# Hybrid attention and delta-rule layer: the delta gates of three groups as half products, another head, other planner constants

## The chip, the core and the metric

The kernel runs on one core of one Trainium2 chip. The metric is the device time of one execution in microseconds (us); the time before is the median of three runs. The engines are TensorE (PE, with its weight loads shown as PEld), VectorE (DVE), ScalarE (ACT), GpSimd (POOL) and SyncE (SP, which issues most DMAs).

## The reference, cut

One decoder layer on 512 tokens of width 1024, with 16 meta tokens in front (528 in all). Attention and a gated delta rule run on the same normalised stream; each is gated, projected, gated again, and merged.

```python
hn = rms_norm(h, norm_w)
proj = hn @ w_in
aq, ak, av, az, dq, dk, dv, dz, db, da, ga, gd = jnp.split(proj, offs, axis=-1)
...
o_a = diff_attention(qa, ka, va, lam)
y_a = (o_a * jax.nn.silu(az)) @ w_branch_attn
...
qkv = jax.nn.silu(causal_depthwise_conv(qkv, conv_w))
o_d = gated_delta_chunked(q, k, v, beta, g)
o_d = rms_norm(o_d[:, pad:], dn_norm_w).reshape(B, L, DN_WIDTH)
y_d = (o_d * jax.nn.silu(dz)) @ w_branch_delta
merged = jax.nn.sigmoid(ga) * y_a + jax.nn.sigmoid(gd) * y_d
return merged @ w_out
```

The layer's output is added to the input and normalised once more; the meta tokens are dropped. All is float32.

## The kernel before

**Dense products.** The columns of w_in are taken in blocks of 128 (one head of aq, ak, av, az, dq, dk, dv or dz, or 128 columns of a merge gate ga or gd). ORDER lists the blocks: four groups of two heads, each with dk, dv, dq, dz and the attention blocks, then gd, ga and the branch products yd and ya. The 1024 rows of a block are 8 pieces of 128. To keep float32 precision, each operand is split into a high and a low part of the faster type float32r (wh and wl for weights, hnH and hnL for the normalised stream), and three products are summed: high by high, high by low, low by high (PASSES). A plain block (`product`) is thus 8 x 3 matmuls for each token segment; for dz, az, aq, ga and gd one segment of 512 tokens (BODY), without the meta tokens.

**Half products.** `pair_of_blocks` computes two neighbouring blocks together, by Strassen's scheme in Winograd's form: the weights of the two blocks, the two halves of the 1024 rows and the two halves of the 528 tokens (264 each) make a 2x2 by 2x2 product, done in seven products in place of eight. Each is 4 pieces x 3 passes of 264 columns. `split_pair` makes the weight sums: four DVE operations of 512 columns, then four high parts on ACT and four low parts on DVE (wa, wb, wc of 1024 columns, wd of 512). The sums over tokens (sumH, sumL) are made once by `token_sums`. Partial results leave PSUM by two snapshots (`snap`) and one into cn (`snap_c`) on ACT, and four additions (`total`) on DVE, into two of four buffers xp (or vT for attention). Then a `whole_...` function takes the block from there. PAIRS says which blocks go this way: before the change ak from the second on, dk, dv and dq of the last three groups, and four blocks of gd.

**The gates of the delta rule.** silu of dz is made as (tanh(z/2) + 1) * z, with the factor one half elsewhere. `after_gate` reads z from PSUM: tanh on ACT into one of two buffers th, then, once the old content of the slot of od has been spilled to DRAM, one DVE operation. The delta rule's output is later multiplied onto it (`steps`).

**The planner.** The program is written by a list scheduler that runs on the host (`Plan`). Every piece of work is a generator that yields what it waits for: an engine, an event, a buffer or a PSUM bank. Of all tasks that wait for an engine, the planner issues the one with the earliest start by its own estimates, and at equal starts the lowest rank. HOP, NEAR, SAME and PE_NS are its estimates of the time from engine to engine and of a matmul's fixed part; BIAS adds to the rank of tasks by name. The order it writes on each engine is fixed; the chip then runs each engine in that order, with semaphores between them. Buffers are limited (SLOTS): four raw weight tiles, three pairs of split weights (W), four xp, two th, six PSUM banks beside two of scores.

**The head.** `loads` issues the DMAs of x (four tiles of 128 tokens), of the meta tokens, and of the first weight blocks. `normalise(n)` does, for the meta tokens (n = 0) and for each tile of x (n = 1 to 4): squares with a sum on ACT, mean and eps on DVE, the power -0.5 on POOL (rs), scaling by rs and by the norm weights on DVE (`half`), transposes on PE, and the split into hnH (ACT) and hnL (DVE) in `part`. The norm weights must stand in all 128 partitions: `norm_weights` multiplies a row of ones by the row nrow on PE, into the PSUM tile psc, after eight products of ones that keep PE going. `first_products` then computes dk of heads 0 and 1, over 272 and then 256 tokens; each block goes through its three passes before the next one starts. Its weights are split in `split`.

All of it is issued through the helper at line 238, so the profile names nearly every instruction by that line; tiles tell them apart. psc is the PSUM tile of scores, room holds the gates od and oa, raw the weights as loaded, st the scratch for squares and for weight sums.

Of the kernel before, what the change touches and what calls it, by code (L numbers as in the profile page):

```python
# [33 lines left out]
def dense_order():  # L34
# [7 lines left out]
    for n in range(KB):  # L42
# [14 lines left out]

ORDER = dense_order()

PAIRS = [n for n, (name, i) in enumerate(ORDER) if name == "ak" and i or name == "gd" and i in range(0, 4, 2) or name in ("dk", "dv", "dq") and i > 1 and i % 2 == 0]  # L60
PAIRED = {m for n in PAIRS for m in (n, n + 1)}
HALF = L // 2
PASSES = ((0, 0), (0, 1), (1, 0))
# [14 lines left out]


COLD = 5200  # L80
HOP = {PE: 205.4, DVE: 130, ACT: 104.2, POOL: 90, SP: 0}
NEAR = {PE: 80, DVE: 0, ACT: 0, POOL: 0, SP: 0}
SAME = 81.7
PE_NS = dict(transpose=53, f32=0.1, f32r=11.2, long=18)
BIAS = dict(after_aq=-1.7, after_dv=-0.5, attention=-0.3, combine=0.3, decayed=2, keys=-0.3, move=-2, norms=-1,
            output=2.5, products=-2, quarter=1, rest=1, split=-0.3, split_pair=-0.5, sums=2, values=2.6, whole_av=-1,
            whole_dk=0.3, whole_dq=2)


class Task:  # L90
    def __init__(self, gen, rank, time, src):
        self.gen, self.rank, self.time, self.src, self.want, self.slot = gen, rank, time, src, (), 0
        self.issued = None


class Plan:
# [8 lines left out]
    def __init__(self, slots, kinds, banks):  # L105
        self.free = dict.fromkeys((PE, DVE, ACT, POOL, SP), 0.0)
        self.slots = {k: [(0.0, SP, i) for i in range(n)] for k, n in slots.items()}
        self.slots["bank"] = [(0.0, SP, i) for i in range(banks)]
        self.kinds = dict(kinds)
        self.events, self.tasks = {}, []  # L110
        self.task, self.engine, self.end, self.arrival = None, None, 0.0, 0.0
        self.dma = self.hwdge = 0.0

# [5 lines left out]

    def spawn(self, gen, rank=None):  # L120
        time, src = self.here() if self.task else (0.0, SP)
        rank = (self.task.rank if rank is None else rank) + BIAS.get(gen.__name__, 0)
        self.tasks.append(Task(gen, rank, time, src))

    def done(self, event):
        self.events[event] = self.here()
# [65 lines left out]
    def run(self):  # L192
        self.settle()
        while self.tasks:
            best = None
            for task in self.tasks:
                eng = task.want
                if isinstance(eng, tuple) or eng not in self.free:
                    continue
                t = task.time if task.issued is None or eng != SP else task.issued  # L200
                if task.src != eng:
                    t += HOP[task.src] + NEAR[eng]
                elif eng in (DVE, ACT):
                    t += SAME
                key = max(t, self.free[eng]), task.rank
# [69 lines left out]
def hybrid_block(ctx: ExitStack, tc: tile.TileContext, x, meta, wblk, wbd, wout, pcol, prow, out):  # L275
# [49 lines left out]
        return ticks[event] == n  # L325


    nrow = mk(sp, [1, D], F32, "nrow")
    nc.scalar.dma_start(out=nrow, in_=prow[:, 1296:2320])
    plan.events["nrow"] = 3200.0, SP  # L330
    mt = mk(sp, [P, 2 * P], F32, "mt")
    plan.free.update({ACT: 2000.0, DVE: 1000.0, POOL: 1200.0, SP: 630.0})

# [81 lines left out]
    def split(n, raw, which):  # L415

        m = n - len(ORDER)
        if m < 0 or m in (4, 5):
            if n:
                yield f"took {n - 1 if m != 4 else len(ORDER) - 1}"  # L420
            yield ("W",)
            w_slot[n] = plan.task.slot
            wh, wl = Ws[plan.task.slot]
            done(f"took {n}")
        else:
            yield ("wo",)
            wo_slot[n] = plan.task.slot
            wh, wl = wos[plan.task.slot]
        if n == 1:
            yield "hh2"  # L430
        yield ACT
        A.copy(out=wh, in_=raw)
        weights[n] = wh, wl
        done(f"wh{n}")
        if n == 0:
            yield "scaled 2"
        yield DVE
        V.tensor_tensor(out=wl, in0=raw, in1=wh.bitcast(F32), op=ALU.subtract)
        plan.give("raw", which)
        done(f"w{n}")  # L440
# [75 lines left out]
    def loads():  # L516
        for n in range(1, NC + 1):
            yield SP
            S.dma_start(out=xt[n], in_=x[P * (n - 1):P * n, :])
            done(f"x{n}")  # L520
# [12 lines left out]
        S.dma_start(out=wbr, in_=wbd)  # L533
        done("wbr")
        for n in range(2, len(ORDER) + 8):
            yield from load_weights(n)


    hn = [hnp.tile([P, KB, L], F32R, tag=t, name=t) for t in ("hnH", "hnL")]

    def normalise(n):

        yield f"x{n}"
# [2 lines left out]
        ss, rs = (mk(sp, [P, 1], F32, t, 5) for t in ("ss", "rs"))  # L546
        if n > 2:
            yield "hh2"
        yield ACT
        A.activation(out=st[:, :w], in_=xt[n], func=AF.Square, accum_out=ss)  # L550
        src = ss
        if n == 0:
            yield "same"
# [5 lines left out]
        yield DVE  # L559
        V.tensor_scalar(out=ss, in0=src, scalar1=1.0 / D, scalar2=EPS, op0=ALU.mult, op1=ALU.add)  # L560
        if n == 0:
            give("pdl", pt)
        yield POOL
# [34 lines left out]
            spawn(part(pt, dst, hf), 0.25 + 0.02 * hf)  # L598

        for hf in range(1 if n == 0 else 2):  # L600
            spawn(half(hf))
# [339 lines left out]
    def after_dq(h, banks):  # L941
        pair["q", h], _ = yield from conv_silu(banks, h, NM, "qT")
        give("y")
        done(f"dq{h}")

    def whole_gd(c, which):
        th = xps[which][:, 3 + NM:3 + L]
# [664 lines left out]
    def attention(h):  # L1612
# [129 lines left out]
        if h < H - RING["oa"]:  # L1742
# [8 lines left out]
    WHOLE = dict(dk=whole_dk, dv=whole_dv, dq=whole_dq, ak=whole_ak, av=whole_av, gd=whole_gd)  # L1751
    parts, th_, mg = {}, {}, {}

    def branch(name, of):
# [180 lines left out]
    def first_products():  # L1935

        dst = [[], []]
        banks = [Banks(n) for n in range(2)]
        for hb, (t0, nn) in enumerate(FULL):
            for n in range(2):  # L1940
                if n == 1 and hb == 1:
                    yield ("psc",)
                    dst[1].append(bank("psc")[:, 0])
                else:
                    yield ("pd",)
                    dst[n].append(bank("pd"))
                pd = dst[n][hb][:, :nn]
                for m, (i, j) in enumerate(((0, 0), (1, 0), (0, 1))):
                    yield (f"wh{n}", f"w{n}")[i]
                    for e in (0, 1, 2) if hb == 0 else (3, 4):  # L1950
                        yield f"{('hh', 'hn')[j]}{e}" + ("/0" if j == 0 else "")
                    for k in range(KB):
                        if j == 0 and k == KB // 2:
                            for e in (1, 2) if hb == 0 else (3, 4):
                                yield f"hh{e}/1"
                        yield PE
                        T.matmul(pd, weights[n][i][:, k * P:(k + 1) * P], hn[j][:, k, t0:t0 + nn],
                                 start=k == 0 and m == 0, stop=k == KB - 1 and m == 2)
# [336 lines left out]
            spawn(delta_pair(gi))  # L2295
            yield "ap"

    for task, rank in ((norm_weights(), 0), (loads(), 0), (constants(), 5), (gates(), 0.6), (deltas(), 0), (pools(), 0), (dense(), 4),
                       (token_sums(), 3), (returns(), 1)):
# [52 lines left out]
```

## Time and profile before

| what | us |
|---|---|
| median of three runs | 748.05 |
| lowest and highest | 748.04, 749.8 |
| the profiled execution's own time | 748.15 |
| its span, first to last instruction | 746.4 |

The profile is of one execution. A busy time is the union of an engine's instructions; those of PE overlap each other, since matmuls are pipelined and their ends are modelled. In a table by stretches the columns are the stretch, its length, and for PE, PEld, DVE, ACT and POOL the busy time with the number of instructions; then the clock granted to PE (1.00 is full), the share of the DMA engines, and GB/s. In a row by group, behind the count stand the busy time and the mean of one in ns, and behind the next bar the idle time of the engine before them and what ended it. In a timeline row stand start, length, engine, line, operation, tiles and count.

### The profile page before, as it was taken

Reading aid. Unit: us, or ns where it says so; the run is one execution under the profiler, and the core shown is the slowest. Engines: PE = TensorE matmul, PEld = TensorE weight load, DVE = VectorE, ACT = ScalarE, POOL = GpSimd, SP = SyncE. Lnnn points to the kernel's source line nnn. Section 1 sums busy time; section 2 is a strip of 40 time slices with the busy share of each in tenths; the row PEclk is TensorE's granted clock in tenths of the full one; section 3 lists DMA queues with packets and bytes.
Section 4 is the critical chain, followed back from the end, with each engine's and each line's share of the span. In section 5 each row is a group of like instructions: output and inputs, shape, how many; then the busy total and the mean of one; then the engine's idle time right before and its main releaser. Section 6 shows DMA issues by size and latency. Waiting matters only on the chain.

```text
span 746.4 us, 14531 instructions
## 1 busy us (share of the span) xinstructions
PE 733.6 (98%) x5346; PEld 670.1 (90%) x5346; DVE 624.0 (84%) x1472; ACT 519.0 (70%) x1390; POOL 64.0 (9%) x72
## 2 busy tenths in 40 slices
PE   8999999999999999999999999999999999999996
PEld 7998988899898899889889989989988999899875
DVE  5989998888899988889997798998569767989553
ACT  6449857899977598987668898768785445555232
POOL 2104001003100002200100220010010000000001
PEclk8999999999999999999999999999999999999998
DMA  8233211424243222432233232403273443215603
GB/s 300 67 108 121 87 57 65 99 74 133 79 126 104 55 71 79 133 114 88 98 66 84 86 118 83 142 29 73 93 249 111 154 158 114 85 57 165 203 1 113
DMA packets 51249, 79.11 MB, mean 106 GB/s; under 512 B 21029, under 2 KB 30685, under 8 KB 51178
## 3 DMA queue, kind: packets, MB, share of 16 engines
q1 hardware_dynamic: 51176, 78.18, 33.0%
q8 instruction: 42, 0.69, 0.4%
q14 instruction: 29, 0.24, 0.1%
q10 hardware_dynamic: 2, 0.00, 0.0%
HBM read 70.63 MB, written 7.55 MB: 105 GB/s over the span
## 4 chain that ended last, share of the span: by engine, by line
PE 73%; DVE 15%; ACT 6%; issue 2%; DMA 1%; POOL 1%; SPq 0%; POOLq 0%; DVEq 0%; ACTq 0%
PE bank L238 70%; DVE wl L238 3%; PE psc L238 3%; DVE room L238 2%; DVE ts L238 1%; DVE psc L238 1%; ACT wh L238 1%; DVE vin L238 1%; ACT ak L238 1%; DMA raw<-in_wblk_dram 1%; DVE y L238 1%; DVE sumL L238 1%; ACT e L238 1%; DVE aq L238 1%; DVE ast L238 1%
## 5 line engine op out<-in xcount | busy, mean ns | idle before, releaser
L238 PE MATMUL bank<-hnH,wh 128*128 128x512 f32 (+4 forms) x624 | 218.7, 356 | 0.2
L238 PE MATMUL bank<-hnL,wh 128*128 128x512 f32 (+4 forms) x624 | 207.0, 336 | 0.2 <-DVE ss L238 0.2
L238 PE MATMUL bank<-hnH,wl 128*128 128x512 f32 (+4 forms) x624 | 206.8, 336 | 0.0
L238 DVE TENSOR_TENSOR wl<-raw,wh 128x1024 fp32r<-128x1024 f32 (+1 forms) x124 | 137.1, 1109 | 21.6 <-ACT wh L238 21.0
L238 ACT CAST wh<-raw 128x1024 fp32r<-128x1024 f32 (+1 forms) x124 | 118.5, 958 | 38.9 <-PE bank L238 30.6
L238 PEld LDWEIGHTS bank<-hnH,wh 128*128 128x128 f32 x624 | 117.5, 191 | 12.5 <-issue 0.3
L238 PEld LDWEIGHTS bank<-hnH,wl 128*128 128x128 f32 x624 | 116.9, 190 | 12.5
L238 PEld LDWEIGHTS bank<-hnL,wh 128*128 128x128 f32 x624 | 116.7, 189 | 9.9 <-DVE ss L238 0.4
L238 PE MATMUL bank<-sumH,wh 128*128 128x264 f32 x288 | 88.8, 308 | 0.0
L238 PE MATMUL bank<-sumH,wl 128*128 128x264 f32 x288 | 81.8, 284 | 0.0
L238 PE MATMUL bank<-sumL,wh 128*128 128x264 f32 x288 | 81.7, 284 | 0.0
L238 DVE SCALAR_TENSOR_TENSOR y<-xp,pc,y 128x528 f32<-128x528 f32 (+1 forms) x72 | 54.3, 758 | 1.6 <-ACT y L238 1.3
L238 PEld LDWEIGHTS bank<-sumH,wh 128*128 128x128 f32 x288 | 54.6, 189 | 0.3
L238 PEld LDWEIGHTS bank<-sumL,wh 128*128 128x128 f32 x288 | 54.5, 189 | 0.0
L238 PEld LDWEIGHTS bank<-sumH,wl 128*128 128x128 f32 x288 | 54.2, 188 | 0.0
L238 ACT ACTIVATE e<-psc,ast 128x144 f32<-128x144 f32 (+3 forms) x64 | 34.6, 542 | 17.9 <-DVE ast L238 16.9
L238 DVE TENSOR_TENSOR wl<-st,wh 128x1024 fp32r<-128x1024 f32 x26 | 31.8, 1222 | 7.7 <-ACT wh L238 7.7
L238 PE MATMUL bank<-btH,wh 128*128 128x256 f32 x128 | 36.3, 284 | 0.5 <-ACT sn L238 0.5
L238 POOL TENSOR_TENSOR ass<-ass,mhalf 128x4 f32<-128x4 f32 x8 | 10.1, 1260 | 306.3 <-DVE ass L238 175.1
L238 PE MATMUL bank<-btH,wl 128*128 128x256 f32 x128 | 36.2, 283 | 0.0
L238 PE MATMUL bank<-btL,wh 128*128 128x256 f32 x128 | 36.1, 282 | 0.0
L238 ACT CAST wh<-st 128x1024 fp32r<-128x1024 f32 x26 | 27.3, 1048 | 11.3 <-PE bank L238 10.8
(382 smaller groups left out, 1722.7 us busy)
## 6 DMA issues: line engine op xcount, KB each, us to landing
raw<-in_wblk_dram SPq DMA_DIRECT2D x96, 512.0 KB, 3.6
raw<-in_wout_dram SPq DMA_DIRECT2D x8, 512.0 KB, 4.7
xt<-in_x_dram SPq DMA_DIRECT2D x4, 512.0 KB, 6.7
TE<-gcd SPq DMA_DIRECT2D x8, 256.0 KB, 4.6
TT<-gcd SPq DMA_DIRECT2D x8, 256.0 KB
xr<-in_x_dram SPq DMA_DIRECT2D x8, 256.0 KB, 6.3
out_dram<-xr SPq DMA_DIRECT2D x7, 256.0 KB, 2.3
room<-scrm SPq DMA_DIRECT2D x12, 128.0 KB, 3.7
```

What stands on the lines that cost most here:

```text
L238: return real(*args, **kw)
```

## The change

It has three parts.

The dz blocks of groups 1 to 3 become pairs: PAIRS takes in dz, and `whole_dz` makes the gate from xp instead of PSUM. The blocks of group 0 stay as they are.

The head: nrow is loaded as 8 rows of 128 and transposed once, copied to SBUF as eight columns (nwc), and each column, repeated along the free axis, is transposed into psc. The eight products of ones go; a task of the highest rank (`keep_busy`) issues such products whenever nothing else of PE is ready in the plan, until the first half of hnH of tile 2 is there. The squares of tile 1 are shared by half between ACT and DVE, those of tile 2 by three quarters and one quarter. Tile 2 goes ahead of the meta tokens. The high part of the first weight block is made in two halves, that of the third block waits until tile 4 is scaled. `first_products` goes through its passes in another order.

The planner's constants: HOP, NEAR, SAME, PE_NS and BIAS have other values, and BOOST changes the rank of two single tasks.

```diff
-PAIRS = [... or name in ("dk", "dv", "dq") and i > 1 and i % 2 == 0]
+PAIRS = [... or name in ("dk", "dv", "dq", "dz") and i > 1 and i % 2 == 0]
...
-HOP = {PE: 205.4, DVE: 130, ACT: 104.2, POOL: 90, SP: 0}
-NEAR = {PE: 80, DVE: 0, ACT: 0, POOL: 0, SP: 0}
-SAME = 81.7
-PE_NS = dict(transpose=53, f32=0.1, f32r=11.2, long=18)
-BIAS = dict(after_aq=-1.7, after_dv=-0.5, attention=-0.3, combine=0.3, decayed=2, keys=-0.3, move=-2, norms=-1,
-            output=2.5, products=-2, quarter=1, rest=1, split=-0.3, split_pair=-0.5, sums=2, values=2.6, whole_av=-1,
-            whole_dk=0.3, whole_dq=2)
+HOP = {PE: 100, DVE: 84.9, ACT: 140, POOL: 90, SP: 0}
+NEAR = {PE: 87.2, DVE: 0, ACT: 0, POOL: 0, SP: 0}
+SAME = 120
+PE_NS = dict(transpose=53, f32=0.5, f32r=10.6, long=15.7)
+BIAS = dict(after_dv=-0.5, after_gate=-2.3, after_sigmoid=1.5, combine=-0.3, decayed=-2.8, delta_pair=-1.5,
+            diagonal=-0.5, evac=2.3, keys=1, part=2.5, queries=0.5, rest=0.3, sigmoid=-2, total=-0.2, whole_ak=0.3,
+            whole_dv=1.5)
+BOOST = {"delta_pair 2": 0.7, "split 14": -0.7}
...
-    nrow = mk(sp, [1, D], F32, "nrow")
-    nc.scalar.dma_start(out=nrow, in_=prow[:, 1296:2320])
-    plan.events["nrow"] = 3200.0, SP
+    nrow = mk(sp, [KB, P], F32, "nrow")
+    nc.scalar.dma_start(out=nrow, in_=prow[:, 1296:2320].rearrange("o (k p) -> (o k) p", p=P))
+    plan.events["nrow"] = 2600.0, SP
...
-        if n == 1:
-            yield "hh2"
-        yield ACT
-        A.copy(out=wh, in_=raw)
+        if n in (1, 2):
+            yield ("hh2", "scaled 4")[n - 1]
         weights[n] = wh, wl
+        if n == 0:
+            yield ACT
+            A.copy(out=wh[:, :D // 2], in_=raw[:, :D // 2])
+            done("wh0/0")
+            plan.task.rank += 0.04
+            yield ACT
+            A.copy(out=wh[:, D // 2:], in_=raw[:, D // 2:])
+        else:
+            yield ACT
+            A.copy(out=wh, in_=raw)
...
+    def other_squares(n, m):
+        late["ss", n] = mk(sp, [P, 1], F32, "sx", 2)
+        yield DVE
+        V.tensor_tensor_reduce(out=st[:, m:], in0=xt[n][:, m:], in1=xt[n][:, m:], scale=1.0 / D, scalar=EPS, op0=ALU.mult,
+                               op1=ALU.add, accum_out=late["ss", n])
+        done(f"squares {n}")
...
+        m = {1: D // 2, 2: D // 4 * 3}.get(n, w)
+        if m < w:
+            spawn(other_squares(n, m))
         yield ACT
-        A.activation(out=st[:, :w], in_=xt[n], func=AF.Square, accum_out=ss)
+        A.activation(out=st[:, :m], in_=xt[n][:, :m], func=AF.Square, accum_out=ss)
...
+        if m < w:
+            yield f"squares {n}"
+            yield DVE
+            V.scalar_tensor_tensor(out=ss, in0=ss, scalar=1.0 / D, in1=late["ss", n], op0=ALU.mult, op1=ALU.add)
...
+        nwc = mk(sp, [P, KB], F32, "nwc")
+        yield "nrow"
         yield PE
-        for _ in range(8):
-            T.matmul(late["nw"][0][:, 0:P], ones, ones, start=True, stop=True)
-        yield "nrow"
-        for hf in range(2):
+        T.transpose(nw[:, 1, 0:KB], nrow, ident[0:KB, 0:KB])
+        yield DVE
+        V.tensor_copy(out=nwc, in_=nw[:, 1, 0:KB])
+        for k in range(KB):
             yield PE
-            T.matmul(late["nw"][hf], ones[0:1], nrow[:, 512 * hf:512 * hf + 512], start=True, stop=True)
-            done(f"norm weights {hf}")
+            T.transpose(nw[:, k // 4, k % 4 * P:k % 4 * P + P], nwc[:, k:k + 1].broadcast_to([P, P]), ident)
+            tick(f"norm weights {k // 4}", 4)
+
+    def keep_busy():
+        yield ("pdl",)
+        fill = bank("pdl")
+        while "hh2/0" not in plan.events:
+            yield PE
+            T.matmul(fill[:, 0:P], ones, ones, start=True, stop=True)
+        give("pdl", fill)
...
+    def whole_dz(h, which):
+        z = xps[which][:, 3 + NM:3 + L]
+        yield ("th",)
+        at_ = plan.task.slot
+        th = ths[at_]
+        yield ACT
+        A.activation(out=th, in_=z, func=AF.Tanh, scale=0.5)
+        if h >= RING["od"]:
+            yield f"od out {h - RING['od']}"
+        yield DVE
+        V.scalar_tensor_tensor(out=gate["od"][h], in0=th, scalar=1.0, in1=z, op0=ALU.add, op1=ALU.mult)
+        plan.give("xp", which)
+        plan.give("th", at_)
+        done(f"dz{h}")
...
-            for n in range(2):
-                if n == 1 and hb == 1:
...
+            for n, m in ((0, 0), (0, 1), (1, 0), (0, 2), (1, 1), (1, 2)):
+                i, j = ((0, 0), (1, 0), (0, 1))[m]
...
-    for n, rank in ((1, 0), (0, 0.1), (2, 0.2), (3, 0.4), (4, 0.5)):
+    for n, rank in ((1, 0), (2, 0.02), (0, 0.04), (3, 0.4), (4, 0.5)):
         spawn(normalise(n), rank)
```

More of the change, by code (lines that the diff above doesn't have):

```diff
@@ L58 @@
 ORDER = dense_order()
-PAIRS = [n for n, (name, i) in enumerate(ORDER) if name == "ak" and i or name == "gd" and i in range(0, 4, 2) or name in ("dk", "dv", "dq") and i > 1 and i % 2 == 0]
+PAIRS = [n for n, (name, i) in enumerate(ORDER) if name == "ak" and i or name == "gd" and i in range(0, 4, 2) or name in ("dk", "dv", "dq", "dz") and i > 1 and i % 2 == 0]
 PAIRED = {m for n in PAIRS for m in (n, n + 1)}
@@ L92, in __init__ @@
         self.gen, self.rank, self.time, self.src, self.want, self.slot = gen, rank, time, src, (), 0
-        self.issued = None
+        self.issued, self.boost = None, 0
 class Plan:
@@ L109, in __init__ @@
         self.kinds = dict(kinds)
-        self.events, self.tasks = {}, []
+        self.events, self.tasks, self.count = {}, [], {}
         self.task, self.engine, self.end, self.arrival = None, None, 0.0, 0.0
@@ L121, in spawn @@
         time, src = self.here() if self.task else (0.0, SP)
-        rank = (self.task.rank if rank is None else rank) + BIAS.get(gen.__name__, 0)
+        name = gen.__name__
+        rank = (self.task.rank if rank is None else rank) + BIAS.get(name, 0)
         self.tasks.append(Task(gen, rank, time, src))
+        self.count[name] = self.count.get(name, -1) + 1
+        self.tasks[-1].boost = BOOST.get(f"{name} {self.count[name]}", 0)
     def done(self, event):
@@ L204, in run @@
                     t += SAME
-                key = max(t, self.free[eng]), task.rank
+                key = max(t, self.free[eng]), task.rank + task.boost
                 if best is None or key < best[0]:
@@ L519, in loads @@
             S.dma_start(out=xt[n], in_=x[P * (n - 1):P * n, :])
+            plan.late(1200 if n == 2 else 0)
             done(f"x{n}")
@@ L558, in normalise @@
             src = pt[:, 0:1]
-        yield DVE
-        V.tensor_scalar(out=ss, in0=src, scalar1=1.0 / D, scalar2=EPS, op0=ALU.mult, op1=ALU.add)
+        if m < w:
+            yield f"squares {n}"
+            yield DVE
+            V.scalar_tensor_tensor(out=ss, in0=ss, scalar=1.0 / D, in1=late["ss", n], op0=ALU.mult, op1=ALU.add)
+        else:
+            yield DVE
+            V.tensor_scalar(out=ss, in0=src, scalar1=1.0 / D, scalar2=EPS, op0=ALU.mult, op1=ALU.add)
         if n == 0:
@@ L600, in normalise @@
         for hf in range(1 if n == 0 else 2):
-            spawn(half(hf))
+            spawn(half(hf), {0: 0.13, 1: 0.1, 2: 0.12}.get(n, plan.task.rank) + 0.02 * hf)
     def norm_weights():
@@ L944, in after_dq @@
         done(f"dq{h}")
+    def whole_dz(h, which):
[7 more added lines that the diff above has]
+            yield f"od out {h - RING['od']}"
+        yield DVE
+        V.scalar_tensor_tensor(out=gate["od"][h], in0=th, scalar=1.0, in1=z, op0=ALU.add, op1=ALU.mult)
+        plan.give("xp", which)
+        plan.give("th", at_)
+        done(f"dz{h}")
     def whole_gd(c, which):
@@ L1750, in hybrid_block @@
                  av=lambda h, banks: to_whole(whole_av, h, banks))
-    WHOLE = dict(dk=whole_dk, dv=whole_dv, dq=whole_dq, ak=whole_ak, av=whole_av, gd=whole_gd)
+    WHOLE = dict(dk=whole_dk, dv=whole_dv, dq=whole_dq, ak=whole_ak, av=whole_av, gd=whole_gd, dz=whole_dz)
     parts, th_, mg = {}, {}, {}
@@ L1939, in first_products @@
         for hb, (t0, nn) in enumerate(FULL):
-            for n in range(2):
-                if n == 1 and hb == 1:
[L1942 to L1946, printed above, removed]
-                pd = dst[n][hb][:, :nn]
[L1948 to L1958, printed above, removed]
+            for n, m in ((0, 0), (0, 1), (1, 0), (0, 2), (1, 1), (1, 2)):
+                i, j = ((0, 0), (1, 0), (0, 1))[m]
+                if m == 0:
+                    if n == 1 and hb == 1:
+                        yield ("psc",)
+                        dst[1].append(bank("psc")[:, 0])
+                    else:
+                        yield ("pd",)
+                        dst[n].append(bank("pd"))
+                pd = dst[n][hb][:, :nn]
+                yield ("wh0/0" if m == n == 0 else f"wh{n}", f"w{n}")[i]
+                for e in (0, 1, 2) if hb == 0 else (3, 4):
+                    yield f"{('hh', 'hn')[j]}{e}" + ("/0" if j == 0 else "")
+                for k in range(KB):
+                    if j == 0 and k == KB // 2:
+                        yield f"wh{n}"
+                        for e in (1, 2) if hb == 0 else (3, 4):
+                            yield f"hh{e}/1"
+                    yield PE
+                    T.matmul(pd, weights[n][i][:, k * P:(k + 1) * P], hn[j][:, k, t0:t0 + nn],
+                             start=k == 0 and m == 0, stop=k == KB - 1 and m == 2)
+                if m < 2:
+                    continue
                 done(banks[n].event(hb))
@@ L2296, in deltas @@
             yield "ap"
-    for task, rank in ((norm_weights(), 0), (loads(), 0), (constants(), 5), (gates(), 0.6), (deltas(), 0), (pools(), 0), (dense(), 4),
+    for task, rank in ((norm_weights(), -1), (keep_busy(), 9), (loads(), 0), (constants(), 5), (gates(), 0.6), (deltas(), 0), (pools(), 0), (dense(), 4),
                        (token_sums(), 3), (returns(), 1)):
         spawn(task, rank)
-    for n, rank in ((1, 0), (0, 0.1), (2, 0.2), (3, 0.4), (4, 0.5)):
+    for n, rank in ((1, 0), (2, 0.02), (0, 0.04), (3, 0.4), (4, 0.5)):
         spawn(normalise(n), rank)
```

## The prediction

> **What bounds the kernel now.** First the page: its span, the busy time of each engine, and the chain of work that ended last.
>
> ```profile
> span 746.4 us, 14531 instructions
> PE 733.6 (98%) x5346; PEld 670.1 (90%) x5346; DVE 624.0 (84%) x1472; ACT 519.0 (70%) x1390; POOL 64.0 (9%) x72
> PE 73%; DVE 15%; ACT 6%; issue 2%; DMA 1%; POOL 1%; SPq 0%; POOLq 0%; DVEq 0%; ACTq 0%
> ```
>
> TensorE (PE) is busy for 98% of the span and carries 73% of the chain; VectorE (DVE) is second in both. A busy PE may still be waiting inside its pipeline, so I next read the busy time by stretches.
>
> ```profile
> 100.00:500.00 400.00, 397.17 (x3067) 366.26 (x3066) 358.55 (x930) 323.34 (x952) 40.56 (x36) 1.00 0.31 92
> ...
> sum 715.00, PE 711.00 PEld 650.82 DVE 608.04 ACT 503.64 POOL 55.94; mean PE 177.75 PEld 162.70 DVE 152.01 ACT 125.91 POOL 13.99
> ```
>
> The columns are PE, weight loads, DVE, ACT, POOL, then the granted PE clock. From 20 to 735 us PE is idle for 715.00 - 711.00 = 4.0 us. So three things can shorten this kernel: less matmul work, a shorter head before 20 us, or those 4.0 us; the tail after 735 us is not edited. The head:
>
> ```profile
> 10.00:15.00 5.00, 4.56 (x21) 4.31 (x21) 4.57 (x7) 3.49 (x7) 0.00 (x0) 0.50 0.93 310
> ```
>
> PE is granted half its clock from 10 to 15 us, just where the first products run.
>
> **The gates as half products (PE).** Each of three pairs of dz blocks drops 2 blocks x 8 x 3 = 48 matmuls of 512 columns and gains 7 products x 4 x 3 = 84 of 264. A duration in the trace overlaps its neighbour, so I take steps from start to start, between rows of one uninterrupted run of PE's timeline:
>
> ```profile
> 558.81 0.40 PE L238 MATMUL bank<-hnH,wh 128*128 128x512 f32 x1
> ...
> 564.37 0.40 PE L238 MATMUL bank<-hnH,wh 128*128 128x512 f32 x1
> ```
> ```profile
> 177.53 0.37 PE L238 MATMUL bank<-sumH,wh 128*128 128x264 f32 x1
> ...
> 181.84 0.28 PE L238 MATMUL bank<-sumH,wl 128*128 128x264 f32 x1
> ```
>
> The first two rows lie 24 matmuls apart: 5.56/24 = 0.2317 us. The other two lie 35 apart: 4.31/35 = 0.1231 us. A pair goes from 48 x 0.2317 = 11.12 to 84 x 0.1231 = 10.34 us, which saves 0.78, and three save 2.3 us. (The gain is not one eighth, since half products also run over the 16 meta tokens that dz skipped.) The Trainium skill, TensorE: Matmul & The Clock Gate, section on the back-to-back issue gap, gives a warm step as columns/2.4 plus 2.5 ns; by that a pair would save 0.91 us and the three 2.7, an estimate from the page; the rows here are slower per column than it, and the measurement decides.
>
> **What the gates add on DVE and ACT.**
>
> ```profile
> L238 DVE TENSOR_TENSOR wl<-raw,wh 128x1024 fp32r<-128x1024 f32 x98 | 119.5, 1221 | 19.6 <-ACT wh L238 19.2
> ...
> L238 DVE TENSOR_TENSOR wl<-raw,wh 128x512 fp32r<-128x512 f32 x26 | 17.8, 686 | 2.0 <-ACT wh L238 1.8
> ...
> L238 DVE SCALAR_TENSOR_TENSOR room<-room,bank 128x512 f32<-128x512 f32 x16 | 11.1, 694 | 0.0
> ...
> L238 DVE TENSOR_TENSOR xp<-bank,cn 128x264 f32<-128x264 f32 x22 | 9.5, 431 | 4.5 <-PE bank L238 3.1 <-ACT cn L238 1.3
> ...
> L238 DVE SCALAR_TENSOR_TENSOR qT<-xp,y 128x512 f32<-128x512 f32 x8 | 5.5, 682 | 0.8 <-ACT xp L238 0.8
> ```
> ```profile
> L238 ACT CAST wh<-raw 128x1024 fp32r<-128x1024 f32 x98 | 102.7, 1048 | 36.4 <-PE bank L238 30.6 <-DVE raw L238 2.3 <-DVE room L238 1.7
> ...
> L238 ACT CAST wh<-raw 128x512 fp32r<-128x512 f32 x26 | 16.1, 620 | 2.5 <-DVE raw L238 2.4
> ...
> L238 ACT ACTIVATE room<-bank 128x512 f32<-128x512 f32 x19 | 11.3, 596 | 0.0
> ...
> L238 ACT COPY xp<-bank 128x264 f32<-128x264 f32 x22 | 8.4, 381 | 2.3 <-PE bank L238 2.0
> ...
> L238 ACT ACTIVATE xp<-y 128x512 f32<-128x512 f32 x8 | 5.0, 629 | 0.7 <-DVE y L238 0.7
> ```
>
> DVE loses, per pair, two splits and two gates from PSUM: 2 x 1.22 + 2 x 0.69 = 3.83 us. It gains four weight sums (half a split's size, so its price), three and a half splits, four totals and two gates from SBUF: 4 x 0.686 + 3 x 1.221 + 0.686 + 4 x 0.431 + 2 x 0.682 = 10.18. Net +6.35 a pair, 19 us in all. ACT goes from 2 x 1.048 + 2 x 0.596 = 3.29 to 3 x 1.048 + 0.620 + 3 x 0.381 + 2 x 0.629 = 6.16: +2.9 a pair (cn's snap priced as the other two). Loads and spills stay as many. The dz pair holds two of the four xp buffers where the block held PSUM banks; the pair of dk behind it takes the other two. The spill of the old od slot is waited for as before.
>
> What hides 6.35 us of DVE? The first three rows are the dz blocks as they stand; the next three run on through the pair behind them; the last is a long stretch.
>
> ```profile
> 241.20:254.30 13.10, 13.10 (x68) 10.92 (x66) 12.66 (x47) 6.74 (x25) 1.80 (x3) 1.00 0.06 21
> 367.60:381.00 13.40, 13.40 (x66) 10.87 (x66) 13.16 (x53) 6.40 (x21) 0.00 (x0) 1.00 0.07 28
> 490.70:505.20 14.50, 14.50 (x79) 12.29 (x78) 14.06 (x55) 8.19 (x27) 2.23 (x3) 1.00 0.00 0
> 241.20:273.00 31.80, 31.65 (x275) 28.37 (x273) 28.44 (x86) 23.50 (x78) 1.80 (x3) 1.00 0.21 51
> 367.60:400.00 32.40, 31.98 (x273) 28.20 (x273) 27.42 (x85) 22.40 (x67) 0.00 (x0) 1.00 0.22 55
> 490.70:523.00 32.30, 32.30 (x279) 29.00 (x278) 29.03 (x94) 24.10 (x79) 2.23 (x3) 1.00 0.19 42
> ```
> ```profile
> 200.00:250.00 50.00, 50.00 (x342) 45.89 (x341) 48.67 (x137) 37.08 (x101) 2.22 (x3) 1.00 0.32 101
> ```
>
> In the dz blocks themselves DVE is nearly full: free 0.4, 0.2 and 0.4 us. To the end of the next pair it has 3.4, 5.0 and 3.3 us free, so 1.4 to 3.1 us of each 6.35 is carried further as lateness. The cover is other DVE work that can slide (attention, the delta rule) while PE takes what is ready. It holds in the last row: DVE 97% busy for 50 us, PE never idle. The bounds of the cost: below, 0 by that row; above, all that the longer stretches don't cover, 3.0 + 1.4 + 3.1 = 7.5 us, or without any sliding 19. Over 100:500 DVE's free time falls from 41.5 to some 24 us; were PE's 2.83 us idle there to grow in that ratio, it would gain 2. I take **+0.8 us**, nearer the 50 us row. ACT's 2.9 us lie in its own gaps: it is busy 6.7 of 13.1, 6.4 of 13.4 and 8.2 of 14.5 us in the dz blocks, so 0; without that cover they would add to DVE's lateness, at most 2.9 each.
>
> **The head.**
>
> ```profile
> 1.15 3.78 PE L238 MATMUL psc<-ones 128*128 128x128 f32 x16 [1.15 <-DVE ones L238]
> ...
> 4.86 2.02 PE L238 MATMUL psc<-nrow,ones 1*128 1x512 f32 x4
> ...
> 7.00 1.41 DVE L238 SCALAR_TENSOR_TENSOR xt<-xt,rs,psc 128x512 f32<-128x512 f32 x2 [1.14 <-PE psc L238]
> ...
> 8.56 1.07 POOL L238 TENSOR_TENSOR rs<-ss,mhalf 128x1 f32<-128x1 f32 x2 [2.06 <-DVE ss L238]
> ...
> 9.66 1.41 DVE L238 SCALAR_TENSOR_TENSOR xt<-xt,rs,psc 128x512 f32<-128x512 f32 x2 [0.17 <-POOL rs L238]
> ...
> 10.46 1.97 PE L238 MATMUL bank<-ident,xt 128*128 128x128 f32 x8 [0.44 <-DVE xt L238]
> ...
> 12.25 2.18 PE L238 MATMUL bank<-hnH,wh 128*128 128x272 f32 x8
> ...
> 17.12 1.17 PE L238 MATMUL bank<-hnH,wh 128*128 128x272 f32 x8
> ...
> 18.34 2.72 DVE L238 SCALAR_TENSOR_TENSOR xt<-xt,rs,psc 128x512 f32<-128x512 f32 x4
> ```
> ```profile
> 7.00:19.00 12.00, 10.57 (x55) 8.92 (x54) 10.18 (x18) 8.39 (x16) 3.40 (x6) 0.72 0.89 320
> ```
>
> Scaling of x1 starts at 7.00, released by the norm-weight matmuls that end at 6.88. Instead come one transpose, a DVE copy and eight transposes. Eight transposes took 1.97 us at half clock in the row at 10.46; so from 4.86 at the latest the weights are there by about 7.3 at half clock, some 1 us sooner at full, and sooner still if the row of weights lands earlier, since the 16 warming matmuls no longer stand before it. Halved squares of x1 make rs earlier as well. I take 6.3 for x1. For x2 the power no longer stands behind that of the meta tokens (two took 1.07, so 0.53 sooner), the squares lose a quarter, and x1's scaling before it is 0.7 earlier: start near 8.2 instead of 9.66. The first matmul then comes near 10.5 instead of 12.25.
>
> Whether that is kept depends on the feed. At full clock the first eight matmuls take 1.2 us as in the row at 17.12, not 2.18; but from 7 to 19 us DVE was busy 10.18 of 12 and the second scaling (x3, x4) came only at 18.34. DVE gets added squares, priced by 0.69 us for 512 columns and half that for 256, and a small copy: 1.2 us, out of 1.8 idle. The fillers use PE only while nothing else is ready in the plan, and one of two pdl banks until the first half of hnH of x2; one filler call is two of the matmuls of ones, of which 16 took 3.78 us, so 0.5 us if it stands before work that came early. Bounds: a loss of 0.5 (late weights, or one filler too many) to a gain of 3 (start and clock both kept). I take **-1.8 us**, the earlier start. Splitting wh0 costs ACT one fixed part, 2 x 0.620 - 1.048 = 0.2 us; the reorder of the first products gives DVE time for the low parts and changes no count.
>
> **The constants** change the order that the planner writes, not the work. The most to gain is the 4.0 us of idle; at the other end a worse order can cost as much. I take 0, with 1.5 us either way.
>
> **The sum.** -2.3 - 1.8 + 0.8 = -3.3 us. The profiled execution took 748.15 us (span 746.4), the median of three is 748.05, so both are one base: **744.7 us**.
>
> **Rivals.**
> 1. *Better still:* head 2.8 us, no DVE price, the new order takes 1 to 2 of the idle: 748.05 - 2.3 - 2.8 - 1.5 = 741.5. For it: the half clock. Chance 0.17.
> 2. *The head doesn't do what it says:* fillers end before the hn tiles come and the clock still falls, or DVE paces the head. Gain 0: 748.05 - 2.3 + 0.8 = 746.6. For it: DVE's 10.18 of 12. Chance 0.11.
> 3. *DVE becomes the bound at the dz pairs, slower than before:* its 6.35 us lateness reaches PE through the weight splits, of which only three buffers stand ahead. With 7.5 us arriving: 748.05 - 4.1 + 7.5 = 751.5; with all 19: 763. It is slower by over 0.3% once 6.3 of the 19 us reach PE. Against it: the row with DVE at 97%. Chance 0.18, more than half of it above 750.3.
> 4. *Weight loads bind.* If loads ran one after another, each half product would cost a load, not 0.123 us.
>
> ```profile
> L238 PEld LDWEIGHTS bank<-sumH,wh 128*128 128x128 f32 x288 | 54.6, 189 | 0.3
> ```
> ```profile
> 204.00:209.00 5.00, 5.00 (x44) 5.00 (x43) 5.00 (x15) 3.08 (x9) 0.00 (x0) 1.00 0.81 252
> ```
>
> At 0.189 us a pair would take 84 x 0.189 = 15.9 instead of 11.12, three +14.3: 748.05 - 1.8 + 0.8 + 14.3 = 761. But 43 loads in 5.00 us of half products are one per 0.116 us: they overlap. Chance 0.02. [...]
>
> **How the numbers follow.** About 0.3%, 2.2 us, is what a measurement can tell from no change. The forecast has 0.52, 0.43 of it below 745.8. Faster: 0.43 + 0.17 = 0.60. Same: 0.09 + 0.11 + 0.08 = 0.28. Slower: 0.10 + 0.02 = 0.12. The range goes from the better case to where the DVE price is some 5 us: 741.2 to 749.5, leaving out about 0.05 below and 0.14 above.
>
> **What would show it.** In the new trace: the rows of 128x512 matmuls fall by 144 and those of 264 rise by 252, steps unchanged; the clock of 10:15 near 1.00; first product near 10.5 and PE unbroken from about 17; DVE busy near 640; PE idle of 20:735 within 3.5 to 6.5. Idle of PE ended by DVE's wl or st in the dz stretches would make me wrong by rival 3; a half clock after 8 us by rival 2.

## The result, and the profile after

| kernel | median of 6 runs, us | lowest, highest | profiled execution, us | span, us |
|---|---|---|---|---|
| before | 749.59 | 748.04, 750.10 | 748.15 | 746.4 |
| changed | 744.72 | 744.22, 745.59 | 744.65 | 742.9 |

Both were timed together on one chip: ratio 0.9937, 95% interval 0.9926 to 0.9947. The change is faster by some 0.6%. The forecast was 744.7 us. Several of its terms were wrong all the same, and cancelled. Two of the six executions of the kernel before took 748.0 us and the others 749.4 to 750.1, so its profiled one is among the fastest: the medians differ by 4.9 us, the profiled executions by 3.5.

The page of the changed kernel, its span and busy times, then the chain:

```profile
span 742.9 us, 14923 instructions
...
PE 731.9 (99%) x5499; PEld 677.3 (91%) x5499; DVE 638.0 (86%) x1507; ACT 522.9 (70%) x1406; POOL 57.9 (8%) x72
...
PE 85%; ACT 9%; DVE 2%; DMA 2%; issue 2%; SPq 0%; POOL 0%; POOLq 0%; DVEq 0%; ACTq 0%
```

PE is still the bound, now with 85% of the chain. DVE works 14 us more (638.0 against 624.0) and yet carries 2% of the chain instead of 15%. The busy time by stretches (PE, weight loads, DVE, ACT, POOL, then PE's clock), the head's stretch first:

```profile
7.00:19.00 12.00, 12.00 (x104) 11.80 (x103) 10.43 (x22) 8.00 (x16) 3.16 (x6) 1.00 0.97 324
...
100.00:500.00 400.00, 397.36 (x3188) 373.46 (x3187) 371.31 (x971) 322.67 (x945) 34.70 (x34) 1.00 0.31 93
...
20.00:735.00 715.00, 711.24 (x5353) 657.37 (x5351) 622.92 (x1471) 510.25 (x1380) 50.97 (x50) 1.00 0.33 101
```

PE's idle time from 20 to 735 us is 715.00 - 711.24 = 3.8 us (4.0 before), and from 100 to 500 us DVE is busy for 371 of 400 us instead of 359 with PE no idler than it was. The groups of PE's instructions, each form apart, first of the kernel before and then of the changed one:

```profile
L238 PE MATMUL bank<-hnL,wh 128*128 128x512 f32 x288 | 114.0, 396 | 0.0
...
L238 PE MATMUL bank<-sumH,wh 128*128 128x264 f32 x288 | 88.8, 308 | 0.0
...
L238 PE MATMUL bank<-hnL,wh 128*128 128x264 f32 x216 | 61.3, 284 | 0.0
```
```profile
L242 PE MATMUL bank<-sumH,wh 128*128 128x264 f32 x336 | 102.9, 306 | 0.0
...
L242 PE MATMUL bank<-hnL,wh 128*128 128x512 f32 x240 | 94.8, 395 | 0.0
...
L242 PE MATMUL bank<-hnL,wh 128*128 128x264 f32 x252 | 71.5, 284 | 0.0
```

Each of the three kinds of 512-column matmul fell from 288 to 240, and the half products rose from 288 and 216 to 336 and 252: 144 fewer and 252 more, as worked out. The mean times are within 2 ns of those before.

Now the head: DVE's timeline of the changed kernel (start, duration), then ACT's, then PE's.

```profile
7.27 1.40 DVE L242 SCALAR_TENSOR_TENSOR xt<-xt,rs,psc 128x512 f32<-128x512 f32 x2
...
11.19 1.40 DVE L242 SCALAR_TENSOR_TENSOR xt<-xt,rs,psc 128x512 f32<-128x512 f32 x2
```
```profile
8.85 0.59 ACT L242 CAST hnH<-bank 128x512 fp32r<-128x512 f32 x1 [3.18 <-PE bank L242]
9.33 0.85 ACT L242 ACTIVATE st<-xt 128x768 f32<-128x768 f32 x1
```
```profile
5.23 1.81 PE L242 MATMUL psc<-ident,nwc 128*128 128x128 f32 x8
...
13.37 1.43 PE L242 MATMUL bank<-hnH,wh 128*128 128x272 f32 x8
...
31.91 0.29 PE L242 MATMUL bank<-hnH,wh 128*128 128x272 f32 x1
```

The norm weights are there at 5.23 + 1.81 = 7.04 us, and x1 is scaled from 7.27 us: later than the 7.00 of before. The squares of x2 on ACT start at 9.33, behind the rounding of x1's first half, which ACT awaited for 3.18 us. In the kernel before they started at 6.22, as its ACT timeline shows:

```profile
6.22 1.06 ACT L238 ACTIVATE st<-xt 128x1024 f32<-128x1024 f32 x1
```

So x2 is scaled at 11.19 instead of 9.66, and the first dense product comes at 13.37 instead of 12.25: later, where I had put 10.5. What the head gained is that PE never stops there and has its full clock: the first eight matmuls took 1.43 us instead of 2.18. The first matmul of the block dv 0 starts at 31.91 us instead of 32.58, 0.67 us earlier. Between the first dense product and dv 0 every kernel of this document does the same 149 matmuls, fillers not counted, so the start of dv 0 tells what a head is worth.

One trace of each kernel is too little for that, though. Two of the experiments below run the same heads again: gates_light has the order of before there, after_light that of the changed kernel. PE's timelines of before, gates_light and after_light:

```profile
32.58 0.29 PE L238 MATMUL bank<-hnH,wh 128*128 128x272 f32 x1
```
```profile
4.86 3.78 PE L238 MATMUL psc<-nrow,ones 1*128 1x512 f32 x4
...
34.38 0.29 PE L238 MATMUL bank<-hnH,wh 128*128 128x272 f32 x1
```
```profile
5.07 1.04 PE L242 MATMUL psc<-ident,nwc 128*128 128x128 f32 x8
...
30.99 0.29 PE L242 MATMUL bank<-hnH,wh 128*128 128x272 f32 x1
```

The old head came 1.80 us later in gates_light, where the norm-weight matmuls took 3.78 us instead of 2.02; the new one 0.92 us earlier in after_light, where the transposes took 1.04 us instead of 1.81.

### The profile page after: what moved, and what is told of

It reads as the page before. It is cut to its first block, busy times and chain, and to the rows that moved or that the text cites. A ratio compares the mean times of both kernels' runs of the same rounds, so it can differ in the third digit from the quotient of the medians.

```text
span 742.9 us, 14923 instructions
## 1 busy us (share of the span) xinstructions
PE 731.9 (99%) x5499; PEld 677.3 (91%) x5499; DVE 638.0 (86%) x1507; ACT 522.9 (70%) x1406; POOL 57.9 (8%) x72
## 4 chain that ended last, share of the span: by engine, by line
PE 85%; ACT 9%; DVE 2%; DMA 2%; issue 2%; SPq 0%; POOL 0%; POOLq 0%; DVEq 0%; ACTq 0%
PE bank L242 81%; PE psc L242 4%; ACT wh L242 2%; ACT TE L242 1%; DMA unit_columns<-ts 1%; ACT ak L242 1%; ACT MT L242 1%; ACT TT L242 1%; DMA gdd<-xp 1%; DVE wl L242 1%; ACT ktd L242 0%; SPq L242 0%; ACT y L242 0%; ACT ao L242 0%; ACT aq L242 0%
## 5 line engine op out<-in xcount | busy, mean ns | idle before, releaser
L242 PE MATMUL bank<-hnH,wh 128*128 128x512 f32 (+4 forms) x612 | 206.6, 342 | 0.6 <-DVE xp L242 0.6
L242 PE MATMUL bank<-hnH,wl 128*128 128x512 f32 (+4 forms) x612 | 197.6, 328 | 0.6 <-DVE wl L242 0.6
L242 PE MATMUL bank<-hnL,wh 128*128 128x512 f32 (+4 forms) x612 | 197.2, 328 | 0.0
L242 PEld LDWEIGHTS bank<-hnH,wl 128*128 128x128 f32 x612 | 113.9, 188 | 11.5 <-DVE wl L242 1.0
L242 PE MATMUL bank<-sumH,wh 128*128 128x264 f32 x336 | 102.9, 306 | 0.0
L242 PE MATMUL bank<-sumH,wl 128*128 128x264 f32 x336 | 95.5, 284 | 0.0
L242 PE MATMUL bank<-sumL,wh 128*128 128x264 f32 x336 | 95.3, 284 | 0.0
L242 PEld LDWEIGHTS bank<-sumH,wh 128*128 128x128 f32 x336 | 63.6, 189 | 0.8 <-issue 0.2
L242 PEld LDWEIGHTS bank<-sumL,wh 128*128 128x128 f32 x336 | 63.6, 189 | 0.0
L242 PEld LDWEIGHTS bank<-sumH,wl 128*128 128x128 f32 x336 | 63.2, 188 | 0.0
L242 DVE CUSTOM_DVE_ANT_0 psc<-psc,masks 128x144 f32<-128x144 f32 (+3 forms) x64 | 32.5, 508 | 2.2 <-PE psc L242 1.8
```

Of the source, the lines that this page charges most:

```text
L242: return real(*args, **kw)
```

## The experiments

First the change in its three parts: G the gates (PAIRS and `whole_dz`), H the head, C the constants (with BOOST). Each kernel below was timed with runs of the kernel before on the same chip (its medians were 749.59, 749.83, 750.03 and 748.68). PE's idle time is that from 20 to 700 us of the profiled execution, and "half clock" the time between there for which the trace's records of the clock have it at 0.5.

| kernel | parts | median, us | ratio to before, 95% | span, us | PE idle, us | half clock, us |
|---|---|---|---|---|---|---|
| before | none | | 1 | 746.4 | 4.0 | 0 |
| head_only | H | 749.59 | 1.0005 (0.9997 to 1.0014) | 747.7 | 6.0 | 0 |
| constants_only | C | 749.56 | 0.9994 (0.9984 to 1.0003) | 747.8 | 3.1 | 0 |
| no_gates | H, C | 748.11 | 0.9978 (0.9967 to 0.9988) | 745.1 | 3.5 | 0 |
| gates_only | G | 765.57 | 1.0218 (1.0202 to 1.0235) | 763.2 | 11.5 | 20.5 |
| old_head | G, C | 760.92 | 1.0152 (1.0129 to 1.0174) | 755.6 | 9.2 | 10.2 |
| no_constants | G, H | 776.36 | 1.0363 (1.0349 to 1.0376) | 774.9 | 22.8 | 13.7 |
| changed | G, H, C | 744.72 | 0.9937 (0.9926 to 0.9947) | 742.9 | 3.8 | 0 |
| same_122 | all, SAME 122 | 758.20 | 1.0117 (1.0101 to 1.0134) | 758.5 | 9.4 | 17.1 |
| hop_act_125 | all, HOP of ACT 125 | 760.08 | 1.0143 (1.0127 to 1.0159) | 758.2 | 14.0 | 6.8 |

**gates_only**: the diff of PAIRS, `whole_dz` and WHOLE alone, on the kernel before.

> The kernel before with the three dz pairs alone. Theory (parts add up, PE bound): matmul work falls by 2.3 us and DVE's 19 us find cover, so 746 to 747 where before is 748 to 749.5, ratio 0.996 to 0.998; the step of a 264-column matmul stays near 0.123 us. Rival (DVE pays): idle of PE in 100:500 grows from 2.8 to over 5 us and the time is that of before or more. Rival (order): it can land anywhere within 2 us of before, since the order of everything behind the first pair changes.

**head_only**: the diff of `loads`, `normalise`, `norm_weights`, `keep_busy`, `split` and `first_products` alone.

> The kernel before with the new head alone. Theory after the first trace: worth 0.7 us, read at the first matmul of dv 0 (32.58 before, 31.9 after), ratio 0.999; clock 1.00 in 10:15. The size in the prediction was 1.8 us. Rival: the head is worth more in the median than in the one profile, because without the fillers the clock in the head falls differently from run to run (before ran from 748.0 to 750.1): then ratio 0.997 and a narrower spread.

**constants_only**: the diff of HOP, NEAR, SAME, PE_NS, BIAS and BOOST alone.

> The kernel before with the planner's new constants and BOOST alone. Theory: they only reorder, 0 with 1.5 us either way, PE idle of 20:735 between 2.5 and 6 us. Rival (the constants carry the gain): ratio 0.996 or less by themselves.

**no_constants**: the changed kernel with the old constants.

> The new kernel with the old constants (gates and head new). Theory: -2.3 - 0.7 = 3 us under before, ratio 0.996. Rival (the constants were fitted to this kernel and are needed): time of before or above, with more idle of PE in 100:500, ended by DVE.

The gates, the only part that takes matmul work away, alone cost 2.2%. The head alone and the constants alone change nothing that can be measured; the 0.999 expected of head_only lies outside its interval. In its trace dv 0 starts at 30.93 us, 1.65 earlier than in that of before, but the rest of the span takes 747.7 - 30.93 = 716.8 us instead of 746.4 - 32.58 = 713.8, with 2.0 us more of idle: in these two traces the order behind the head lost more than the head gained. Gates and head together cost 3.6%. So the parts don't add up, and a term for the constants of "0, with 1.5 either way" can't be right beside the gates. In gates_only PE is idle for 8.3 us of 100:500, so there the rival in which DVE pays held; in no_constants the rival held by which the constants are needed. In gates_only PE stands and then runs at half clock; its busy time by stretches:

```profile
270.00:275.00 5.00, 2.65 (x21) 2.21 (x19) 4.96 (x11) 4.27 (x15) 0.00 (x0) 0.99 0.47 33
275.00:280.00 5.00, 4.17 (x15) 3.02 (x16) 4.43 (x8) 3.08 (x9) 0.00 (x0) 0.50 0.08 15
280.00:285.00 5.00, 5.00 (x46) 4.47 (x47) 1.37 (x3) 3.23 (x10) 0.00 (x0) 0.50 0.24 90
...
405.00:410.00 5.00, 2.81 (x15) 2.09 (x14) 5.00 (x12) 3.62 (x12) 0.00 (x0) 0.80 0.28 40
410.00:415.00 5.00, 4.40 (x20) 3.76 (x19) 4.88 (x9) 2.59 (x9) 0.00 (x0) 0.52 0.56 123
```

While PE stands, DVE is busy for all of the 5 us: PE waits for something that DVE has not come to. Behind both the clock is halved. The sum for the span: 11.5 - 4.0 = 7.5 us of idle, up to 20.5 / 2 = 10.2 us of half clock, and 2.3 us of matmul work less make 15.4 of the 16.8 us that the span is longer.

**old_head** is the changed kernel with the head of before, **no_gates** the changed kernel with the dz blocks as before.

> The new kernel with the old head (gates and new constants). Theory now: the gates alone cost 16 us because DVE comes late, PE stands for 2 to 5 us and its clock is then halved for 7 to 14 us; the new constants give an order that spreads DVE's work. So here 745 to 747, PE idle of 100:500 under 4 us, the clock at 1.00 from 20 us on. Rival (the order is a draw that happened to suit one kernel, and any change of it, such as the head, breaks it): 755 to 775, with a halved clock somewhere behind 240 us.

> The new kernel with the dz blocks as plain blocks (head and new constants). Theory: DVE has its old room, so the order matters little: 747 to 750, and the gates' worth beside it is the 2.3 us of PE. Rival: 743 or less, that is, the gates cost time even in the new order.

**same_122** and **hop_act_125** change one figure of the planner each, and so the order of the same work:

```diff
-SAME = 120
+SAME = 122
...
-HOP = {PE: 100, DVE: 84.9, ACT: 140, POOL: 90, SP: 0}
+HOP = {PE: 100, DVE: 84.9, ACT: 125, POOL: 90, SP: 0}
```

> The new kernel with one of the planner's estimates moved by 2 ns (SAME 120 to 122), which gives another order of much of the work behind 30 us. Theory (the new constants spread DVE's work by their sense): within 2 us of 744.7. Rival (a draw): over 750, with PE idle behind 240 us ended by DVE and a halved clock.

> The new kernel with another estimate moved (HOP of ACT 140 to 125), a second draw of the order. Theory: within 2 us of 744.7. Rival (a draw): over 750, as above.

no_gates came as its theory had it; in old_head, same_122 and hop_act_125 the theories failed and the rivals held. The table now falls in two. Without the gates, four orders lie within 748 to 750 us. With the gates, the changed kernel takes 744.7 and five other orders take 758 to 776, all with stands and half clock. What the constants give is one order in which the gates do no harm; the two neighbouring settings that were tried don't give it.

Then I kept the order fixed and changed what DVE does in it: the planner's accounts stay as they were, and only the instruction that is written differs.

**gates_light** (on gates_only) and **after_light** (on the changed kernel) thin the sums and low parts of the dz pairs:

```diff
+        def sub(out, in0, in1, op=ALU.subtract):
+            w = 8 if ORDER[n][0] == "dz" else out.shape[1]
+            plan.spend(DVE, V.time("tensor_tensor", (), dict(out=out, in0=in0, in1=in1, op=op)))
+            nc.vector.tensor_tensor(out=out[:, :w], in0=in0[:, :w], in1=in1[:, :w], op=op)
...
-            V.tensor_tensor(out=st[:, h0], in0=a2[:, h0], in1=a2[:, h1], op=ALU.add)
+            sub(out=st[:, h0], in0=a2[:, h0], in1=a2[:, h1], op=ALU.add)
```

> The gates alone (the before kernel's constants and head, the order of gates_only instruction for instruction), with the weight sums and the low parts of the three dz pairs done on 8 columns only: 8 instructions of a pair shrink from 0.68 to 1.22 us each to some 0.07, about 6.5 us of DVE work less per pair. It leaves most of these sums and low parts undone. Theory (DVE's lateness at the dz pairs makes PE stand, and the halved clock after each stand multiplies it): PE's stands of 2 to 5 us near 270 and 405 us go, no stretch at half clock behind them, 745 to 750 us. Rival (this order is slow by itself, by banks and slots that PE waits for, whatever DVE's work takes): 762 to 766 us, with the same stretches at half clock.

gates_light took 762.18 us (761.90 to 762.61), ratio 1.0176 (1.0163 to 1.0189). The theory fell and the rival held. A thinned instruction took 0.16 us where 0.07 had been expected, and DVE's busy time fell from 634.6 to 620.2 us, by 14.4 and not the 20 of the expectation; that brings about 3 us of the 16, by the ratios 1.0218 and 1.0176. The stand near 270 us is still there, with half clock behind it. DVE's timeline of gates_light shows what PE waits for, then ACT's and PE's:

```profile
266.32 0.68 DVE L455 TENSOR_TENSOR st<-raw 128x512 f32<-128x512 f32 x1
...
267.81 0.76 DVE L238 SCALAR_TENSOR_TENSOR y<-xp,pc,y 128x528 f32<-128x528 f32 x1
...
269.75 2.12 DVE L238 SCALAR_TENSOR_TENSOR y<-xp,pc,y 128x528 f32<-128x528 f32 x3
...
272.90 0.76 DVE L238 SCALAR_TENSOR_TENSOR y<-xp,pc,y 128x528 f32<-128x528 f32 x1
273.58 0.69 DVE L455 TENSOR_TENSOR st<-st,raw 128x512 f32<-128x512 f32 x1
```
```profile
274.30 1.05 ACT L238 CAST wh<-st 128x1024 fp32r<-128x1024 f32 x1
```
```profile
275.40 0.39 PE L238 MATMUL bank<-sumH,wh 128*128 128x264 f32 x1 [2.00 <-ACT wh L238]
```

These weights are not those of the dz pair but of dv 4, two pairs further on, and so not thinned. DVE's queue has the second half of their sum `st` 7.3 us behind the first, with convolution steps (y) and softmax work between. ACT can round `st` only then, at 274.30, and PE, which is done with the rest, waits 2.00 us for it. In the changed kernel the same steps stand so (DVE, ACT, and PE's next product with a wh of that kind):

```profile
253.31 0.68 DVE L242 TENSOR_TENSOR st<-raw 128x512 f32<-128x512 f32 x1
...
254.82 0.69 DVE L242 TENSOR_TENSOR st<-st,raw 128x512 f32<-128x512 f32 x1
```
```profile
262.13 1.05 ACT L242 CAST wh<-st 128x1024 fp32r<-128x1024 f32 x1
```
```profile
267.17 0.37 PE L242 MATMUL bank<-sumH,wh 128*128 128x264 f32 x1
```

The two halves are 1.5 us apart, and the rounded weights are there 4 us before PE takes them. At this stand it is the place in DVE's queue that counts. For dv 6, near 405 us in gates_only, the two sums show the same: they start at 398.30 and 407.78 there, at 376.79 and 377.57 in the changed kernel. But the first stands near 405 wait for softmax work (pm, pmT, e), not for these weights.

> The changed kernel, its order kept instruction for instruction, with the same thinning: sums and low parts of the three dz pairs on 8 columns, which leaves most of them undone; some 20 us of DVE work less. Theory (in this order DVE's work for the gates lies beside PE's): within 0.7 us of the changed kernel, 744.0 to 745.5. Rival (the gates' DVE work still costs some of what my forecast put at 0.8 us or more): 742 to 743.8 us.

after_light took 745.51 us (745.22 to 747.14), ratio 0.9957 (0.9944 to 0.9969), at the edge of what the theory gave and on the far side of the rival: taking the DVE work away from the good order gains nothing. (Its head came earlier, as shown above; from dv 0 on its span takes 743.4 - 30.99 = 712.4 us, the changed kernel's 742.9 - 31.91 = 711.0. A stand of 1.3 us behind ACT's pmT, near 194 us, makes most of that; why it is there is not shown.)

**after_dve_more** adds DVE work to the same order:

```diff
+        for _ in range(2):
+            nc.vector.scalar_tensor_tensor(out=gate["od"][h], in0=th, scalar=1.0, in1=z, op0=ALU.add, op1=ALU.mult)
```

> The changed kernel in its own order, with the last gate instruction of each of the six dz blocks of the pairs done three times instead of once: 12 more DVE instructions at 0.681 us, 8.2 us in all, 2.7 per pair, put into DVE's queue and into no plan. Theory (DVE has little room left at these pairs, and a late DVE makes PE stand and halves its clock): 747 to 756 us with at least one stretch at half clock behind a dz pair. Rival (in this order DVE runs well ahead of PE): 744.5 to 745.3 us and no such stretch.

One of its six executions took 1834.94 us; it is left out, and no trace of it was kept. The other five took 750.21 (the profiled one) to 755.06 us, median 752.46; the ratio is 1.0060 (1.0043 to 1.0077). The theory held. Behind the last dz pair, from its stretches and PE's timeline:

```profile
505.00:509.00 4.00, 4.00 (x35) 3.98 (x35) 3.92 (x9) 3.17 (x13) 0.96 (x1) 1.00 0.88 157
509.00:512.00 3.00, 1.62 (x13) 1.36 (x11) 2.87 (x6) 1.48 (x4) 0.00 (x0) 1.00 0.02 3
512.00:517.00 5.00, 5.00 (x34) 4.36 (x33) 4.87 (x10) 2.73 (x7) 1.01 (x1) 0.66 0.00 0
```
```profile
511.53 0.39 PE L242 MATMUL bank<-hnH,wh 128*128 128x264 f32 x1 [1.38 <-DVE xp L242]
```

8.2 us of DVE work cost 5.6 us in the profiled execution (span 748.5 against 742.9; counted from dv 0, which came at 30.92, 6.6) and more in the others: 8.3 us of idle from 20 to 700 us instead of 3.8, and 3.4 us at half clock. So 2.7 us per pair were more than the order had to spare.

**no_fillers** leaves out the products of ones in the head, each still accounted for in the plan:

```diff
-            T.matmul(fill[:, 0:P], ones, ones, start=True, stop=True)
+            plan.spend(PE, T.time("matmul", (fill[:, 0:P], ones, ones), {}) * (2 if plan.end < COLD else 1))
```

> The changed kernel in its own order without the 28 products of ones that keep PE busy in the head; everything else is where it was. Theory (the head's gain is a clock that is full before the first dense product): the granted clock rises later than at 6.8 us and is below full for some of 10 to 20 us, 745.5 to 748 us. Rival (the clock would be full by then from the transposes alone, or the first dense product comes earlier with PE free of these products): 744.0 to 745.0 us.

It took 746.11 us (745.18 to 747.44), ratio 0.9961 (0.9949 to 0.9974); the spread overlaps the changed kernel's. PE's timeline of no_fillers:

```profile
13.15 2.00 PE L242 MATMUL bank<-hnH,wh 128*128 128x272 f32 x8
14.99 1.17 PE L242 MATMUL bank<-hnH,wl 128*128 128x272 f32 x8
```

Without the fillers the first eight matmuls come 0.22 us earlier and take 2.00 us instead of 1.43. dv 0 starts at 32.21 us, 0.30 later than in the trace of the changed kernel and 1.2 later than in the two other traces of its head with fillers (30.99 in after_light, 30.92 in after_dve_more). The theory's mechanism is seen. From dv 0 on both kernels take 711.0 us, so the head makes all of the difference between the two traces; how much of the 1.4 us between the medians it makes, one trace can't say. (The views print a clock of 1.00 for 5:15 of no_fillers, but the trace's records of the clock begin at 14.78 us. Ahead of that eight transposes take 1.97 us, as they did in the kernel before where its clock is recorded at half.)

## Why the prediction was right, and where it was not

**Matmul work, -2.3 us: right.** The counts came out exactly and the mean times of the rows are within 2 ns. The spans of no_gates and the changed kernel, which share head and constants, differ by 745.1 - 742.9 = 2.2 us, and counted from dv 0, which leaves the head out, by 713.3 - 711.0 = 2.3. (Their medians differ by 3.4 us; the profiled execution of no_gates is one of its fastest.)

**DVE's work for the gates, +0.8 us: mis-sized, and the reason half wrong.** In the shipped order it cost nothing: PE's idle time fell by 0.2 us, and after_light gained nothing. But the row that I leaned on, 50 us with DVE at 97% and PE never idle, shows what one order does. I priced the work by how much of it there is; the runs give the same work a different price in each of six orders. My third rival named a path that was seen at one stand, lateness that reaches PE through the split weights, but it too priced the amount of work, and gates_light, with 14.4 us less of it, gained only 3. That its 751.5 to 763 us holds three of the five other orders, with two above it, is then no support for that price. I had left out that a stand of PE can be paid twice, in the stand and in the halved clock behind it.

**The head, -1.8 us: the path was wrong; the size is not shown to be.** The step that failed is that x2's scaling would start near 8.2 us and the first product near 10.5. In the eight traces of the new head with its fillers x2 is scaled at 9.72 to 11.19 us and the first product comes at 12.19 to 13.37. I let x2's squares begin as before and only shrink. In the changed kernel the planner put them behind x1's rounding in ACT's queue, 3.1 us later than they had been. A line of the change that is not shown above tells the planner that x2 arrives 1200 ns later (`plan.late`), but that it is the cause is not shown: head_only has it too, and there the squares stand ahead of that rounding, at 7.93 us. x1 is scaled at 6.38 to 7.27 us, near the 6.3 that I took where the transposes ran at full clock, as in after_light (6.47), and near the 7.3 for half clock in the changed kernel's trace.

What did come is the other half of the argument, full clock and an unbroken PE. From the first product to dv 0 the new head takes 18.5 to 18.8 us, the old one, in five traces, 19.7 to 20.4. dv 0 starts at 30.92 to 31.91 us with the new head and at 32.31 to 34.48 with the old one; the two profiled kernels give 0.67 us, the middle values of the two groups (31.15 and 32.72) 1.6.

**The constants, "change the order, not the work", 0 with 1.5 either way: the step that was wrong.** I bounded a worse order by the 4.0 us for which PE is idle in the kernel before. That bound belongs to the work of before. With the gates, the old constants give 776.36 us: by the medians the new ones are worth 31.6 us beside gates and head, and nothing by themselves (0.9994).

**The sum** was -3.3 us and the profiled executions differ by 748.15 - 744.65 = 3.5: -2.3 of matmul work, -0.67 of the head, -0.2 of idle, and some 0.3 us that I can't assign. In this pair the head and DVE's price erred by about 1 us each, in opposite directions. The medians differ by 4.9 us: my base of 748.05, the median of three executions, was 1.5 us under that of six, and the change was worth 1.6 more than I forecast. That the two cancel to 744.72 is luck. The number could be right at all because the order that came with the change is a good one, which no row of before could show.

**What stays open**: the place in the queue was followed for one stand, by reading the timelines; no run moved a single instruction and left the rest. In the other orders PE stood behind other products of DVE and ACT (its longest waits: qT with 4.9 us in hop_act_125, e with 3.2 in old_head, btH with 2.6 in no_constants, xp with 1.7 in same_122). Why these constants and not their neighbours give a good order was not tried, nor why the same head comes earlier or later from trace to trace.

## What to carry to other kernels

Where a planner writes the order, a change of the work and the planner's constants are one change: price them together, and time the part that saves work with several orders before it is called good or bad. When a full engine gets more work, don't ask how busy it is on average; look up where the instruction that the bound engine waits for stands in its queue, and what has been put before it. And size a kernel's head from several traces: here the same head moved by up to 1.8 us from one to the next.

## What the runs showed that I had not expected

Short stands of PE that lie close together, in the middle of the kernel, are followed by half the clock. The waits of PE in gates_only (us in total, times, longest) begin with

```profile
PE bank L238 <- ACT wh L238: 2.4, 2, 2.0
PE bank L238 <- DVE wl L238: 2.2, 3, 0.8
```

No stand in that run was longer than the 2.0 us near 273, yet 13.65 us at half clock follow it, and 6.83 follow a row of stands below 1 us each near 405 (2.81 of 5 us busy). Every stretch at half clock between 20 and 700 us, in all these traces, lasts 3.41, 6.83, 10.24 or 13.65 us: one to four times 3.41. In after_dve_more one stand of 1.38 us was followed by 3.41 us at half clock; one of 1.6 us, by its waits, was not. In the four kernels without the gates PE's stands are at most 1.1 us long and lie far apart, and none is followed by half clock. The Trainium skill, TensorE: Matmul & The Clock Gate, section HAM oscillation, warns of gaps of PE longer than about 3.4 us. In gates_only and after_dve_more no gap was as long, so by that rule the clock would have stayed full there; the measurement decides. (In hop_act_125 one stand was longer, 4.9 us near 350, and half clock came with it.) A cluster of short stands costs more than its own length: gates_only has 7.5 us more of idle than before and up to 10.2 us of lost clock.
